# Input projections of a hybrid attention and recurrence layer by Strassen's block products

## The chip, the cores and the metric

The kernel runs on one core of one Trainium2 chip. The time is the device time of one execution in microseconds (us), as the median of several runs. TensorE (PE in the profile) does the matrix products, VectorE (DVE), ScalarE (ACT) and GpSimd (POOL) the work on elements, SyncE (SP) issues most of the DMA transfers. SBUF is the memory on the chip that all engines read, PSUM the one that TensorE writes, and DRAM lies outside.

## The reference

One layer: a combined input projection of 2048 tokens, two groups of heads that work on its columns, an output projection with a residual and a layer norm.

```python
h = jnp.einsum('btd,de->bte', h_res, w_in[layer])          # 2048 x 1024 by 1024 x 3328
hq, hf, hi, hg, aq, ak, av, ag = jnp.split(h, IN_SPLITS, axis=-1)
f = lb + (1.0 - lb) * jax.nn.sigmoid(hf)
o_h = hgrn2_chunk(rs(silu(hq)), rs(1.0 - f), rs(hi), rs(jnp.log(f)))   # 4 heads of 128, chunks of 64
...                                                        # norm of o_h, times silu(hg)
q_a = partial_rope(aq ...)                                  # 8 query heads of 64
k_a = partial_rope(ak ...)                                  # 2 key/value heads
o_a = swa_with_sinks(q_a, k_a, v_a, sinks) * silu(ag)       # causal window of 128 tokens
out = jnp.einsum('bte,ed->btd', concat(o_h, o_a), w_out[layer])
z = DN_ALPHA * h_res + out
...                                                        # layer norm of z
```

All is float32. The input projection has 26 column tiles of 128: 10 for attention (kv, two q, two gate tiles for each of the two key/value heads) and 16 for the recurrence (for each of two head pairs: four tiles of forget gate and query, four of value and output gate).

## The kernel before

Each large product is done in three passes. `load_split` fetches 128x1024 of x or of a weight (L94, SyncE), ScalarE copies it to the rounded type (L97, the high part, `_h`), and VectorE or GpSimd subtracts that from the original (L98, the low part, `_l`). Then high by high, high by low and low by high are summed in PSUM. `project_t` (L104 to L112) does that for one weight tile and 512 tokens: 8 slices of the contraction, three matmuls of 128x512 each, 24 in all. `project_n` (L114 to L122) does it with tokens as rows for values and output gates (`vg`).

The work is emitted in three parts. Attention (L184 to L330) runs over the two key/value heads j and over four blocks b of 512 tokens. For each it loads and splits x, projects `kvp`, two `qp` and two `gp`, rotates keys and queries (`rotate`, L206 to L213: VectorE reads PSUM, GpSimd multiplies `sw` by the sines), and goes through four blocks of 128 tokens: scores `sp` (L270, L271), mask and maximum on VectorE (L274 to L280), exponentials on ScalarE (L283), their normalization on GpSimd (L293), four transposes `pt` (L296), two masked copies `ptb` (GpSimd L307, VectorE L317), the product with the values `op` (L320), the gate (L328), and a transfer to DRAM (`sw_spill`, L329).

The recurrence (L354 to L506) runs over two head pairs j and four blocks b. For each head it projects the forget gate `fp` (L380), takes tanh, scans and a reciprocal (`e`, `re`, L382 to L395), makes `kq` on GpSimd (L398, L399), projects the query `hq` (L405), and then goes over two pairs of 128-token blocks: `vg` by `project_n` (L427), in-chunk products `ap`, `kp` (L444, L447, L450), state products `hkv` (L475) and outputs `ho`. The weights of `vg` (`wh_4` to `wh_7`) are loaded at b = 0, with their low parts on GpSimd (L418).

The output part (L509 to L555) does the last product `po` (L537 to L539), the residual, and the norm. The order on each engine is set by a scheduler that works on the whole program; a tile that is written again waits for the readers of what it held. Products take their PSUM tiles from a ring of three (`mm`), scores from another of three (`sc`).

Of the kernel before, what the change touches and what calls it, by code (L numbers as in the profile page):

```python
# [17 lines left out]
P = 128  # L18
# [3 lines left out]
TB = 512  # L22
# [14 lines left out]


@with_exitstack
def tile_hybrid_layer(  # L40
# [17 lines left out]
    rawp = ctx.enter_context(tc.tile_pool(name="rawp", bufs=3))  # L58
    wp = ctx.enter_context(tc.tile_pool(name="wp", bufs=8))
    xp = ctx.enter_context(tc.tile_pool(name="xp", bufs=7))  # L60
# [10 lines left out]
    ]  # L71

    def mm_ps(name):
        return psp.tile([P, 512], F32, tag="mm", name=name, bufs=3)

    def sc_ps(name):
        return psp.tile([P, 512], F32, tag="sc", name=name, bufs=3)
# [9 lines left out]
    def load_split(src, pool, tag, name, scale=None, lo_eng="d", parts=1, stage=None):  # L87
        spool, stag = stage or (rawp, "raw")
        raw = spool.tile([P, 1024], F32, tag=stag, name=f"{name}_raw")
# [13 lines left out]

    def project_t(ps, w, xs):  # L104
        wh, wl = w
        for k in range(KT):
            xh, xl = xs[k // 2]
            c = slice((k % 2) * TB, (k % 2 + 1) * TB)
            r = slice(k * P, (k + 1) * P)
            nc.tensor.matmul(ps, lhsT=wh[:, r], rhs=xh[:, c], start=k == 0, stop=False)  # L110
            nc.tensor.matmul(ps, lhsT=wh[:, r], rhs=xl[:, c], start=False, stop=False)  # L111
            nc.tensor.matmul(ps, lhsT=wl[:, r], rhs=xh[:, c], start=False, stop=k == KT - 1)  # L112
# [69 lines left out]
    hk = ctx.enter_context(tc.tile_pool(name="shared", bufs=2))  # L182
    early = [hk.tile([P, NBLK, 129], F32, tag=f"e{h}", name=f"e{h}_0", bufs=1) for h in range(2)]
    with tc.tile_pool(name="swa", bufs=2, reuse_waits="tile") as wk:  # L184
        for j in range(2):
            wg = [None] * 5
            prev_k = prev_v = None
            for b in range(NTB):
                if j == b == 0:
                    xs = []  # L190
                    for step in ("w0", "x0", "x1", "w1", "x2", "x3", "w2"):
                        i = int(step[1])
                        if step[0] == "w":
                            st_ = (None, (wk, "gate"), (wk, "gate"))[i] if i < 3 else None
                            wg[i] = load_split(wt[i], wp, "w", f"wa0_{i}", parts=2 if i == 0 else 1, stage=st_)
                        else:
                            st_ = None if i < 2 else (hk, "q0")
                            xs.append(load_split(xt[0, i], xp, "x", f"xa0_0_{i}", parts=2, stage=st_))
                else:
                    if wg[0] is None:  # L200
                        wg[0] = load_split(wt[5 * j], wp, "w", f"wa{j}_0")
                    xs = load_x(b, f"xa{j}")
                cs = wk.tile([P, 2, TB], F32, tag="cs", name=f"cs{j}_{b}", bufs=1)
                nc.sync.dma_start(cs, rope[b])

                def rotate(ps, rows, name):  # L206
                    sw = hk.tile([P, TB], F32, tag="sw", name=f"sw_{name}")
                    rot = hk.tile([P, TB], F32, tag="rot", name=f"rot_{name}")
                    nc.vector.stream_shuffle(sw[:rows], ps[:rows], swap)
                    nc.gpsimd.tensor_mul(sw[:rows], sw[:rows], cs[:rows, 1, :])  # L210
                    nc.vector.tensor_mul(rot[:rows], ps[:rows], cs[:rows, 0, :])
                    nc.vector.tensor_add(rot[:rows], rot[:rows], sw[:rows])
                    return rot  # L213

                kvp = mm_ps(f"kvp{j}_{b}")
                project_t(kvp, wg[0], xs)
                kv = hk.tile([P, TB], F32, tag="kv", name=f"kv{j}_{b}", bufs=1)
                nc.scalar.activation(kv, kvp, AF.Copy)
                krot = rotate(kvp, 64, f"k{j}_{b}")
                kh = wk.tile([P, P + TB], F32R, tag="kh", name=f"kh{j}_{b}")  # L220
                kl = wk.tile([P, P + TB], F32R, tag="kl", name=f"kl{j}_{b}")
                if prev_k is not None:
                    for new, old in zip((kh, kl), prev_k):
                        nc.vector.tensor_copy(new[:, 0:P], old[:, TB : TB + P].bitcast(F32))
                nc.scalar.activation(kh[0:64, P:], krot[0:64], AF.Copy)
                nc.scalar.activation(kh[64:128, P:], krot[0:64], AF.Copy)
                nc.vector.tensor_sub(kl[0:64, P:], krot[0:64], kh[0:64, P:].bitcast(F32))
                nc.scalar.activation(kl[64:128, P:], kl[0:64, P:].bitcast(F32), AF.Copy)
                vt = tr_ps(f"vt{j}_{b}")
                for i in range(NBLK):  # L230
                    nc.tensor.transpose(vt[:, i, :], kv[:, i * P : (i + 1) * P], ident)
                v = wk.tile([P, NBLK, 64], F32, tag="v", name=f"v{j}_{b}")
                nc.scalar.activation(v, vt[:, :, 64:128], AF.Copy, scale=0.5)

                qs = []
                for g in range(2):
                    if wg[1 + g] is None:
                        wg[1 + g] = load_split(wt[5 * j + 1 + g], wp, "w", f"wa{j}_{1 + g}")
                    qp = mm_ps(f"qp{j}_{b}_{g}")
                    project_t(qp, wg[1 + g], xs)  # L240
                    qrot = rotate(qp, P, f"q{j}_{b}_{g}")
# [384 lines left out]
```

## Time and profile before

| | |
|---|---|
| median of three runs | 952.93 us (950.11, 952.93, 953.89) |
| span of the profiled execution | 951.3 us |
| TensorE busy | 933.0 us, 98% |
| VectorE busy | 607.3 us, 64% |
| GpSimd busy | 322.0 us, 34% |
| ScalarE busy | 308.4 us, 32% |
| DRAM read, written | 73.41 MB, 16.78 MB |

The span is the time from the first to the last recorded instruction of one execution; the runs' times are taken outside and include what lies around it. A page of the profile gives busy times over the whole span. Below it stand views of stretches (windows), of single instructions in order of time (timeline), of groups of like instructions, and the chain of work that ended last, which is followed back from the last instruction to what released it.

### The profile page before, as it was taken

What the parts mean: (1) busy time and instruction counts of PE and PEld (TensorE: products, weight loads), DVE (VectorE), ACT (ScalarE), POOL (GpSimd) and SP (SyncE); (2) the same over time, 40 slices, a digit from 0 to 9 for tenths busy, and PEclk for the clock granted to TensorE, in tenths of its full rate; (3) what the DMA queues carried; (4) which work ended last, traced back from release to release, by engine and by line L of the source; (5) the groups of instructions that cost most, each with busy time, mean ns of one, the idle gap of its engine ahead of it and who ended that gap; (6) DMA issues with size and microseconds to landing.
All of it is one profiled execution on the core that took longest, in us unless ns stands there. A gap on an engine that the chain in (4) does not pass through costs nothing.

```text
span 951.3 us, 12917 instructions
## 1 busy us (share of the span) xinstructions
PE 933.0 (98%) x4744; PEld 750.7 (79%) x4744; DVE 607.3 (64%) x1233; ACT 308.4 (32%) x785; POOL 322.0 (34%) x306
## 2 busy tenths in 40 slices
PE   8999999999998999999999999999999989999996
PEld 7878777777786777878887887888788878888885
DVE  5877887867879955726366383726458446666554
ACT  5455545544564423131142423122133211000000
POOL 1645536445447534313042642313133111111111
PEclk9999999999999999999999999999999999999998
DMA  7423243033242403002032321103013253444321
GB/s 261 165 72 123 70 158 124 33 106 106 78 151 94 127 12 101 23 12 100 1 122 78 100 100 65 47 1 102 10 56 123 78 188 134 143 152 146 113 99 57
DMA packets 33216, 91.03 MB, mean 96 GB/s; under 512 B 4224, under 2 KB 12416, under 8 KB 33152
## 3 DMA queue, kind: packets, MB, share of 16 engines
q1 hardware_dynamic: 27792, 73.41, 23.7%
q0 software_dynamic: 2912, 8.40, 2.5%
q10 hardware_dynamic: 2448, 8.39, 2.2%
q8 instruction: 37, 0.61, 0.3%
q14 instruction: 27, 0.22, 0.1%
HBM read 73.41 MB, written 16.78 MB: 95 GB/s over the span
## 4 chain that ended last, share of the span: by engine, by line
PE 85%; DVE 6%; DMA 4%; ACT 3%; issue 1%; SPq 0%; POOL 0%; POOLq 0%; DVEq 0%; ACTq 0%
PE vg L121 6%; PE vg L120 6%; PE vg L122 6%; PE po L537 6%; PE po L539 6%; PE po L538 6%; PE fp L110 3%; PE fp L111 3%; PE fp L112 3%; PE hq L112 3%; PE hq L110 3%; PE hq L111 3%; PE op L320 3%; PE qp L112 2%; PE qp L110 2%; PE qp L111 2%
## 5 line engine op out<-in xcount | busy, mean ns | idle before, releaser
L537 PE MATMUL po<-wo_h,mh 128*128 128x512 f32 (+1 forms) x264 | 103.1, 391 | 2.8 <-DVE z L540 2.8
L539 PE MATMUL po<-wo_h,ml 128*128 128x512 f32 (+1 forms) x264 | 102.0, 386 | 0.0
L538 PE MATMUL po<-wo_l,mh 128*128 128x512 f32 (+1 forms) x264 | 101.9, 386 | 0.0
L120 PE MATMUL vg<-wh_h,xh_h 128*128 128x512 f32 x256 | 100.8, 394 | 0.0
L121 PE MATMUL vg<-wh_l,xh_h 128*128 128x512 f32 x256 | 100.8, 394 | 0.0
L122 PE MATMUL vg<-wh_h,xh_l 128*128 128x512 f32 x256 | 100.7, 394 | 0.0
L98 POOL TENSOR_TENSOR xh_l<-xh_raw,xh_h 128x1024 fp32r<-128x1024 f32 x16 | 39.1, 2448 | 125.6 <-ACT xh_h L97 122.9
L540 DVE SCALAR_TENSOR_TENSOR z<-xr,po 128x512 f32<-128x512 f32 (+1 forms) x33 | 22.1, 672 | 70.3 <-PE po L539 64.3
L545 POOL TENSOR_SCALAR rs<-mv 128x1 f32<-128x1 f32 x16 | 9.4, 584 | 151.4 <-DVE mv L543 151.4
L283 ACT ACTIVATE wt<-sp,st 128x128 f32<-128x128 f32 x128 | 45.8, 365 | 44.4 <-DVE st L279 44.0
L537 PEld LDWEIGHTS po<-wo_h,mh 128*128 128x128 f32 x264 | 50.1, 190 | 12.4 <-DVE z L540 3.0
L293 POOL TENSOR_TENSOR wt<-wt,st 128x512 f32<-128x512 f32 x32 | 37.4, 1169 | 61.9 <-DVE st L292 35.2
L539 PEld LDWEIGHTS po<-wo_h,ml 128*128 128x128 f32 x264 | 50.0, 189 | 10.1
L538 PEld LDWEIGHTS po<-wo_l,mh 128*128 128x128 f32 x264 | 50.0, 189 | 9.5
L343 ACT ACTIVATE mh<-mp 128x512 fp32r<-128x512 f32 x16 | 9.6, 599 | 144.8 <-PE mp L342 144.8
L120 PEld LDWEIGHTS vg<-wh_h,xh_h 128*128 128x128 f32 x256 | 48.4, 189 | 10.1 <-issue 0.6
L121 PEld LDWEIGHTS vg<-wh_l,xh_h 128*128 128x128 f32 x256 | 48.1, 188 | 10.2 <-issue 0.6
L122 PEld LDWEIGHTS vg<-wh_h,xh_l 128*128 128x128 f32 x256 | 48.1, 188 | 9.9 <-issue 0.4
L395 DVE RECIPROCAL re<-e 128x512 f32<-128x512 f32 x16 | 53.5, 3344 | 0.0
L433 DVE SCALAR_TENSOR_TENSOR hg<-tg,vg 128x256 f32<-128x256 f32 x32 | 13.4, 420 | 60.2 <-ACT tg L431 60.2
L110 PE MATMUL fp<-xh_h,wh_h 128*128 128x512 f32 x128 | 51.2, 400 | 0.0
L110 PE MATMUL qp<-xa_h,wa_h 128*128 128x512 f32 x128 | 50.7, 396 | 0.0
(173 smaller groups left out, 2483.9 us busy)
## 6 DMA issues: line engine op xcount, KB each, us to landing
xh_raw<-in_xt_dram SPq DMA_DIRECT2D x32, 512.0 KB, 3.6
xa_raw<-in_xt_dram SPq DMA_DIRECT2D x28, 512.0 KB, 3.7
wh_raw<-in_wt_dram SPq DMA_DIRECT2D x16, 512.0 KB, 3.4
xr<-in_xn_dram SPq DMA_DIRECT2D x16, 512.0 KB, 3.6
out_dram<-y ACTq DMA_DIRECT2D x15, 512.0 KB, 2.6
wa_raw<-in_wt_dram SPq DMA_DIRECT2D x9, 512.0 KB, 4.9
cs<-in_rope_dram SPq DMA_DIRECT2D x8, 512.0 KB, 3.4
sw_spill<-mix POOLq DMA_DIRECT2D x32, 128.0 KB, 2.5
```

Source lines behind the costliest of these rows:

```text
L98: engines[lo_eng].tensor_sub(lo[:, c], raw[:, c], hi[:, c].bitcast(F32))
L110: nc.tensor.matmul(ps, lhsT=wh[:, r], rhs=xh[:, c], start=k == 0, stop=False)
L111: nc.tensor.matmul(ps, lhsT=wh[:, r], rhs=xl[:, c], start=False, stop=False)
L112: nc.tensor.matmul(ps, lhsT=wl[:, r], rhs=xh[:, c], start=False, stop=k == KT - 1)
L120: nc.tensor.matmul(ps, lhsT=xh[:, r], rhs=wh[:, c], start=k == 0, stop=False)
L121: nc.tensor.matmul(ps, lhsT=xh[:, r], rhs=wl[:, c], start=False, stop=False)
L122: nc.tensor.matmul(ps, lhsT=xl[:, r], rhs=wh[:, c], start=False, stop=k == KT - 1)
L283: nc.scalar.activation(wt_[:, s, :], sps[s // 2][:, s % 2, P:], AF.Exp, bias=st[:, 1, s : s + 1], scale=0.125, accum_out=st[:, 3, s : s + 1],)
L395: nc.vector.reciprocal(re, e[:, :, 1:129])
L537: nc.tensor.matmul(ps, lhsT=mh[:, e, :], rhs=wh[:, c], start=e == 0, stop=False)
L538: nc.tensor.matmul(ps, lhsT=mh[:, e, :], rhs=wl[:, c], start=False, stop=False)
L539: nc.tensor.matmul(ps, lhsT=ml[:, e, :], rhs=wh[:, c], start=False, stop=e == 7)
```

## The change

18 of the 26 column tiles, all of attention's ten and the eight of forget gates and queries, are paired (`PAIRS`). For a pair of tiles and a half of the tokens (1024) the product is cut in 2 by 2 blocks: contraction halves of 512, token blocks of 512, tiles of 128 columns. Strassen's scheme gives the four result blocks from seven block products, with sums of blocks of x (`s1` to `s4`, and the plain `a11`, `a12`, `a22`) and of blocks of the weights (`t1` to `t4`). Each block product is 12 matmuls of 128x512, against 8 x 12 in the plain way. Three PSUM tiles `px`, `py`, `pz` take the products; ScalarE copies their interim sums to SBUF (`snap`, L300 after the change), VectorE adds the other half (`joined`, L308), and SyncE stores each result block of 128x512 in DRAM (`proj`, 72 blocks of 256 KB).

There are 18 steps: two token halves with nine pairs each. The x factors are made once a half (`prepare_x`), 28 blocks split in high and low parts, 16 of them sums that VectorE makes; each has one buffer, so the second half's are written over the first's. The weight factors are made for each step (`prepare_w`), seven blocks; the low parts go to VectorE and GpSimd in turn. The four attention units of a half (`attend`) are emitted at steps 3 to 6 of it, and read their projections from DRAM. The recurrence starts behind all steps, reads `fp` and `qp` from DRAM and keeps `project_n` for `vg`; its pools lie in the SBUF memory that the steps' pools had. Products and scores share a ring of six PSUM tiles. Lines of the changed kernel are not those of the profile.

```diff
+PAIRS = [(0, 5), (1, 2), (3, 4), (6, 7), (8, 9), (10, 12), (11, 13), (18, 20), (19, 21)]
...
+    proj = {
+        (w, b): dram.tile([P, TB], F32, tag=f"pj{w}_{b}", name=f"proj{w}_{b}")
+        for pair in PAIRS
+        for w in pair
+        for b in range(NTB)
+    }
     def mm_ps(name):
-        return psp.tile([P, 512], F32, tag="mm", name=name, bufs=3)
+        return psp.tile([P, 512], F32, tag="mm", name=name, bufs=6)
     def sc_ps(name):
-        return psp.tile([P, 512], F32, tag="sc", name=name, bufs=3)
+        return psp.tile([P, 512], F32, tag="mm", name=name, bufs=6)
...
+        def split2(src, h, l):
+            nc.scalar.activation(h, src, AF.Copy)
+            lo_engine().tensor_sub(l, src, h.bitcast(F32))
...
+        def prepare_x(s):
...
+            def put(n, q, src):
+                h = xc.tile([P, 512], F32R, tag=f"{n}{q}h", name=f"x{s}_{n}{q}h")
+                l = xc.tile([P, 512], F32R, tag=f"{n}{q}l", name=f"x{s}_{n}{q}l")
+                split2(src, h, l)
+                made[n][q] = (h, l)
...
+            for q in range(4):
+                a21, a22 = load(1, q, f"x{s}_r21{q}"), load(1, 4 + q, f"x{s}_r22{q}")
+                a11, a12 = load(0, q, f"x{s}_q11{q}"), load(0, 4 + q, f"x{s}_q12{q}")
+                s1, s2 = tmp_tile(f"x{s}_s1{q}"), tmp_tile(f"x{s}_s2{q}")
+                nc.vector.tensor_add(s1, a21, a22)
+                nc.vector.tensor_sub(s2, s1, a11)
+                put("s2", q, s2)
+                put("s1", q, s1)
+                s3 = tmp_tile(f"x{s}_s3{q}")
+                nc.vector.tensor_sub(s3, a11, a21)
+                put("s3", q, s3)
+                s4 = tmp_tile(f"x{s}_s4{q}")
+                nc.vector.tensor_sub(s4, a12, s2)
+                put("s4", q, s4)
+                put("a22", q, a22)
...
+        def prepare_w(s, pair, raws):
+            b11, b12, b21, b22 = raws
+            w = {1: w_split(b11, f"{n}_1"), 2: w_split(b21, f"{n}_2")}
+            nc.vector.tensor_sub(t1, b12, b11)
+            nc.vector.tensor_sub(t2, b22, t1)
+            w[6] = w_split(t2, f"{n}_6")
+            w[5] = w_split(t1, f"{n}_5")
+            nc.gpsimd.tensor_sub(t3, b22, b12)
+            w[7] = w_split(t3, f"{n}_7")
+            w[3] = w_split(b22, f"{n}_3")
+            nc.gpsimd.tensor_sub(t4, b21, t2)
+            w[4] = w_split(t4, f"{n}_4")
...
+            px = mm_ps(f"px{n}")
+            product(px, w[1], x["a11"], True)
+            s1 = snap(px, "s1")
+            py = mm_ps(f"py{n}")
+            product(py, w[2], x["a12"], True)
+            joined(0, 0, py, s1)
+            product(px, w[6], x["s2"], False)
+            s2 = snap(px, "s2")
+            pz = mm_ps(f"pz{n}")
+            product(pz, w[5], x["s1"], True)
+            s5 = snap(pz, "s5")
+            product(px, w[7], x["s3"], False)
+            joined(1, 1, px, s5)
+            product(pz, w[3], x["s4"], False)
+            joined(0, 1, pz, s2)
+            product(px, w[4], x["a22"], False)
+            finish(1, 0, snap(px, "c10"))
...
-                project_t(kvp, wg[0], xs)
+            kv = fetch(0, "kvc", 1)
...
+        ready = {3: (0, 0), 4: (0, 1), 5: (1, 0), 6: (1, 1)}
+        for t, (s, pair) in enumerate(steps):
...
+            if t + 1 < len(steps):
+                ahead = load_pair(*steps[t + 1])
+                w_next = prepare_w(*steps[t + 1], ahead)
+            if t % len(PAIRS) in ready:
+                j, half = ready[t % len(PAIRS)]
+                attend(j, 2 * s + half)
+            multiply(s, pair, w, x)
...
-                    fp = mm_ps(f"fp{hd}_{b}")
-                    project_t(fp, wf[2 * h], xs)
+                    fp = hk.tile([P, TB], F32, tag="fp", name=f"fp{hd}_{b}")
+                    nc.sync.dma_start(fp, proj[10 + 8 * j + 2 * h, b])
...
-                    qp = mm_ps(f"hq{hd}_{b}")
-                    project_t(qp, wf[2 * h + 1], xs)
+                    qp = hk.tile([P, TB], F32, tag="qp", name=f"qp{hd}_{b}")
+                    nc.sync.dma_start(qp, proj[11 + 8 * j + 2 * h, b])
```

Three places show how the order moves. On VectorE near the start, before the change, low parts of weights and x stand ahead of the first rotations of key and query.

```order
L98 TENSOR_TENSOR wa_2_l<-wa_2_raw,wa_2_h 128x1024
L98 TENSOR_TENSOR wa_3_l<-wa_3_raw,wa_3_h 128x1024
L98 TENSOR_TENSOR wa_4_l<-wa_4_raw,wa_4_h 128x1024
L209 STREAM_SHUFFLE sw_k_0_277<-kvp_0_250 64x512
L211 TENSOR_TENSOR rot_k_0_278<-kvp_0_250,cs_0_248 64x512
L209 STREAM_SHUFFLE sw_q_0_0_321<-qp_0_0_296 128x512
L211 TENSOR_TENSOR rot_q_0_0_322<-qp_0_0_296,cs_0_248 128x512
L98 TENSOR_TENSOR xa_1_0_l<-xa_1_0_raw,xa_1_0_h 128x1024
L212 TENSOR_TENSOR rot_k_0_278<-rot_k_0_278,sw_k_0_277 64x512
```

After the change there stand at that place the sums of x blocks (`x_s`), low parts of factors, and the join of the first result block (`c_0_0`).

```order
L189 TENSOR_TENSOR x_a220l<-x_r_341,x_a220h 128x512
L247 TENSOR_TENSOR x_s_344<-x_s_343,xk_263 128x512
L189 TENSOR_TENSOR x_s20l<-x_s_344,x_s20h 128x512
L189 TENSOR_TENSOR x_a222l<-x_r_405,x_a222h 128x512
L251 TENSOR_TENSOR x_s_355<-xk_263,x_r_339 128x512
L308 TENSOR_TENSOR c_0_0_539<-py_0_526,s_0_0_524 128x512
L189 TENSOR_TENSOR x_s30l<-x_s_355,x_s30h 128x512
L189 TENSOR_TENSOR w_0_3l<-w_5_1_261,w_0_3h 128x512
L254 TENSOR_TENSOR x_s_361<-xk_319,x_s_344 128x512
L246 TENSOR_TENSOR x_s_375<-x_r_371,x_r_373 128x512
```

So the first steps of VectorE went from a few subtractions for one block of tokens to the whole set of factors of 1024 tokens.

On GpSimd, before the change, the low parts of the `vg` weights are made among attention's last blocks (`sw_q` of the rotation, `ptb`, `wt`, and a spill).

```order
L98 TENSOR_TENSOR wh_4_l<-wh_4_raw,wh_4_h 128x1024
L210 TENSOR_TENSOR sw_q_3_0_3058<-sw_q_3_0_3058,cs_3_2983 128x512
L307 AFFINE_SELECT ptb_8_0_2810<-wtt_8_2808 128x512
L210 TENSOR_TENSOR sw_q_3_1_3094<-sw_q_3_1_3094,cs_3_2983 128x512
L98 TENSOR_TENSOR wh_5_l<-wh_5_raw,wh_5_h 128x1024
L293 TENSOR_TENSOR wt_10_2867<-wt_10_2867,st_10_2868 128x512
L307 AFFINE_SELECT ptb_9_0_2856<-wtt_9_2854 128x512
L329 DMA sw_spill_1_89<-mix_8_2818 128x256
L98 TENSOR_TENSOR wh_6_l<-wh_6_raw,wh_6_h 128x1024
```

After the change they stand at the start of the recurrence, between `k` and `kq` of the first two blocks of tokens and low parts of x.

```order
L102 TENSOR_TENSOR xh_0_1_l<-xh_0_1_raw,xh_0_1_h 128x1024
L542 TENSOR_SCALAR k_0_5333<-thf_0_5329,nc_242,c_241 128x512
L554 TENSOR_TENSOR kq_0_5345<-k_0_5333,e_0_5291 128x4x64
L102 TENSOR_TENSOR xh_0_3_l<-xh_0_3_raw,xh_0_3_h 128x1024
L555 TENSOR_TENSOR kq_0_5345<-k_0_5333,re_0_5343 128x4x64
L102 TENSOR_TENSOR wh_4_l<-wh_4_raw,wh_4_h 128x1024
L542 TENSOR_SCALAR k_0_5362<-thf_0_5358,nc_242,c_241 128x512
L102 TENSOR_TENSOR wh_5_l<-wh_5_raw,wh_5_h 128x1024
L554 TENSOR_TENSOR kq_0_5374<-k_0_5362,e_0_5293 128x4x64
L102 TENSOR_TENSOR wh_6_l<-wh_6_raw,wh_6_h 128x1024
L555 TENSOR_TENSOR kq_0_5374<-k_0_5362,re_0_5372 128x4x64
L102 TENSOR_TENSOR wh_7_l<-wh_7_raw,wh_7_h 128x1024
```

So attention's operations no longer stand around them.

On TensorE, before the change, the first `vg` product follows the last query projection `hq` of its block.

```order
L110 MATMUL hq_0_3530<-xh_0_3_h,wh_3_h 128x512
L111 MATMUL hq_0_3530<-xh_0_3_l,wh_3_h 128x512
L112 MATMUL hq_0_3530<-xh_0_3_h,wh_3_l 128x512
L120 MATMUL vg_0_0_3585<-wh_4_h,xh_0_0_h 128x512
L121 MATMUL vg_0_0_3585<-wh_4_l,xh_0_0_h 128x512
L122 MATMUL vg_0_0_3585<-wh_4_h,xh_0_0_l 128x512
```

After the change it follows the last Strassen product (`px_19`, of the pair 19 and 21), and first pieces of two `vg` tiles stand ahead of `kp` and `ap`, which need `kq`.

```order
L292 MATMUL px_19_5168<-x_a223l,w_19_4h 128x512
L293 MATMUL px_19_5168<-x_a223h,w_19_4l 128x512
L114 MATMUL vg_0_0_5409<-wh_4_h,xh_0_0_h 128x512
L114 MATMUL vg_0_1_5440<-wh_4_h,xh_0_0_h 128x512
L608 MATMUL kp_0_0_5472<-ident,kq_0_5345 128x128
L598 MATMUL ap_0_0_5471<-kq_0_5345 64x128
L601 MATMUL ap_0_0_5471<-kq_0_5345 64x64
L115 MATMUL vg_0_0_5409<-wh_4_l,xh_0_0_h 128x512
L116 MATMUL vg_0_0_5409<-wh_4_h,xh_0_0_l 128x512
```

So the recurrence's first TensorE instructions now stand directly behind the last step of the products, with no projection of the same block in between.

## Rows read from the trace of the kernel before

**Rows 1.** The page: span, busy time of each engine, chain that ended last.
```profile
span 951.3 us, 12917 instructions
PE 933.0 (98%) x4744; PEld 750.7 (79%) x4744; DVE 607.3 (64%) x1233; ACT 308.4 (32%) x785; POOL 322.0 (34%) x306
...
PE 85%; DVE 6%; DMA 4%; ACT 3%; issue 1%; SPq 0%; POOL 0%; POOLq 0%; DVEq 0%; ACTq 0%
```
**Rows 2.** Timeline of TensorE, dense stretch: start us, duration us, engine, line, instruction.
```profile
484.04 0.40 PE L111 MATMUL fp<-xh_l,wh_h 128*128 128x512 f32 x1
...
489.06 0.39 PE L112 MATMUL fp<-xh_h,wh_l 128*128 128x512 f32 x1
```
**Rows 3.** Windows 50:300: all; L110; L296 (PE, PEld); L98 (DVE, POOL).
```profile
50.00:300.00 250.00, 248.73 (x1314) 195.22 (x1313) 198.73 (x439) 131.84 (x366) 126.82 (x108) 1.00 0.30 100
...
50.00:300.00 250.00, 103.71 (x263) 49.48 (x263) 1.00 0.30 100
...
50.00:300.00 250.00, 16.66 (x104) 12.46 (x104) 1.00 0.30 100
...
50.00:300.00 250.00, 33.24 (x21) 35.26 (x14) 1.00 0.30 100
```
A row of a window gives the stretch and its length, busy us and instructions of PE, PEld, DVE, ACT and POOL (of one line only the engines that it runs on), granted TensorE clock, DMA share, GB/s.

**Rows 4.** Window of one recurrence step, all engines.
```profile
418.70:472.80 54.10, 54.10 (x283) 43.79 (x282) 27.26 (x60) 12.86 (x34) 14.28 (x14) 1.00 0.15 49
```
**Rows 5.** Chain of work: same instruction in two steps (start us, duration us).
```profile
418.73 0.44 PE hkv L475 x4
...
472.83 0.44 PE hkv L475 x4
```
**Rows 6.** TensorE's timeline at the start; first data of x on ScalarE.
```profile
8.30 0.49 PE L110 MATMUL kvp<-xa_h,wa_h 128*128 128x512 f32 x1 [0.55 <-ACT xa_h L97]
...
14.23 0.39 PE L112 MATMUL kvp<-xa_h,wa_l 128*128 128x512 f32 x1
...
L97 ACT ACTIVATE xa_h<-xa_raw x15: 615/635/1063, 7.6 to 46.8; 128x512 fp32r<-128x512 f32 x8, 128x1024 fp32r<-128x1024 f32 x7
```
**Rows 7.** Groups by shape: busy us, mean ns of one, idle time before.
```profile
L98 DVE TENSOR_TENSOR xa_l<-xa_raw,xa_h 128x512 fp32r<-128x512 f32 x8 | 5.2, 684 | 3.8 <-ACT xa_h L97 3.8
...
L98 POOL TENSOR_TENSOR wh_l<-wh_raw,wh_h 128x1024 fp32r<-128x1024 f32 x8 | 19.6, 2449 | 0.1
...
L386 POOL TENSOR_SCALAR k<-thf,nc,c 128x512 f32<-128x512 f32 x16 | 19.0, 1188 | 38.5 <-ACT thf L382 38.5
...
L398 POOL TENSOR_TENSOR kq<-k,e 128x256 f32<-128x256 f32 x16 | 13.4, 835 | 25.5 <-DVE e L392 25.4
...
L97 ACT ACTIVATE xh_h<-xh_raw 128x1024 fp32r<-128x1024 f32 x32 | 33.7, 1059 | 26.5 <-DMA xh_raw<-in_xt_dram 22.0 <-PE vg L121 4.5
```
**Rows 8.** Timeline of VectorE and GpSimd, 25 to 33 us.
```profile
25.09 2.76 POOL L210 TENSOR_TENSOR sw_q<-sw_q,cs 128x512 f32<-128x512 f32 x1
...
26.61 1.78 DVE L212 TENSOR_TENSOR rot_k<-rot_k,sw_k 64x512 f32<-64x512 f32 x1
27.79 4.59 POOL L98 TENSOR_TENSOR xa_l<-xa_raw,xa_h 128x1024 fp32r<-128x1024 f32 x1
28.31 0.68 DVE L212 TENSOR_TENSOR rot_q<-rot_q,sw_q 128x512 f32<-128x512 f32 x1
28.92 1.21 DVE L98 TENSOR_TENSOR xa_l<-xa_raw,xa_h 128x1024 fp32r<-128x1024 f32 x1
```
**Rows 9.** A wait of TensorE in its timeline, and the window behind it.
```profile
309.79 0.38 PE L270 MATMUL sp<-kh,q 128*128 128x256 f32 x1 [1.85 <-ACT wt L283]
...
310.80:314.20 3.40, 3.40 (x11) 2.82 (x11) 3.04 (x7) 3.40 (x5) 3.11 (x3) 0.50 0.13 49
```
**Rows 10.** DMA issues: count, KB each, median us from issue to landing.
```profile
sw_spill<-mix POOLq DMA_DIRECT2D x32, 128.0 KB, 2.5
```

More of the change, by code (lines that the diff above doesn't have):

```diff
@@ L57, in tile_hybrid_layer @@
     const = ctx.enter_context(tc.tile_pool(name="const", bufs=1))
-    rawp = ctx.enter_context(tc.tile_pool(name="rawp", bufs=3))
-    wp = ctx.enter_context(tc.tile_pool(name="wp", bufs=8))
-    xp = ctx.enter_context(tc.tile_pool(name="xp", bufs=7))
     psp = ctx.enter_context(tc.tile_pool(name="psp", bufs=2, space=PSUM))
@@ L85, in tile_hybrid_layer, with load_split @@
     engines = {"d": nc.vector, "p": nc.gpsimd}
-    def load_split(src, pool, tag, name, scale=None, lo_eng="d", parts=1, stage=None):
-        spool, stag = stage or (rawp, "raw")
-        raw = spool.tile([P, 1024], F32, tag=stag, name=f"{name}_raw")
+    def load_split(src, pool, tag, name, scale=None, lo_eng="d", parts=1):
+        raw = rawp.tile([P, 1024], F32, tag="raw", name=f"{name}_raw")
         hi = pool.tile([P, 1024], F32R, tag=f"{tag}h", name=f"{name}_h")
@@ L102, in load_x @@
         return [load_split(xt[b, j], xp, "x", f"{name}_{b}_{j}", lo_eng=LO_ENGINES[j]) for j in range(4)]
[L104 to L112, printed above, removed]
     def project_n(ps, ws, xs, blk):
@@ L351, in load_wo @@
         return load_split(wo[e], pool, tag, f"wo{e}", scale=hgw_s[:, e : e + 1] if e < 4 else None)
+    late = ctx.enter_context(ExitStack())
+    rawp = late.enter_context(tc.tile_pool(name="rawp", bufs=3, reuse_waits="tile"))
+    wp = late.enter_context(tc.tile_pool(name="wp", bufs=8, reuse_waits="tile"))
+    xp = late.enter_context(tc.tile_pool(name="xp", bufs=7, reuse_waits="tile"))
     with (
@@ L357, in tile_hybrid_layer @@
     ):
-        es = [[early[h], wk1.tile([P, NBLK, 129], F32, tag=f"e{h}", name=f"e{h}_1")] for h in range(2)]
+        hk = wk
+        es = [
+            [wk1.tile([P, NBLK, 129], F32, tag=f"e{h}_{i}", name=f"e{h}_{i}") for i in range(2)] for h in range(2)
+        ]
         ats = [wk1.tile([P, 4, P], F32, tag=f"at{i}", name=f"at{i}") for i in range(2)]
@@ L364, in tile_hybrid_layer @@
         for j in range(2):
-            wf = [None] * 4
             wv = None
@@ L369, in tile_hybrid_layer @@
             for b in range(NTB):
-                if b == 0:
-                    wf[0] = load_split(wt[10 + 8 * j], wp, "w", f"wh{j}_0")
                 xs = load_x(b, f"xh{j}")
@@ L376, in tile_hybrid_layer @@
                     e = es[h][b % 2]
-                    if b == 0 and h == 1:
-                        wf[2] = load_split(wt[10 + 8 * j + 2], wp, "w", f"wh{j}_2")
-                    fp = mm_ps(f"fp{hd}_{b}")
-                    project_t(fp, wf[2 * h], xs)
+                    fp = hk.tile([P, TB], F32, tag="fp", name=f"fp{hd}_{b}")
+                    nc.sync.dma_start(fp, proj[10 + 8 * j + 2 * h, b])
                     th = hk.tile([P, TB], F32, tag="th", name=f"thf{hd}_{b}", bufs=2)
@@ L400, in tile_hybrid_layer @@
                     kn.append(knh)
-                    if b == 0:
-                        wf[2 * h + 1] = load_split(wt[10 + 8 * j + 2 * h + 1], wp, "w", f"wh{j}_{2 * h + 1}")
-                    qp = mm_ps(f"hq{hd}_{b}")
-                    project_t(qp, wf[2 * h + 1], xs)
+                    qp = hk.tile([P, TB], F32, tag="qp", name=f"qp{hd}_{b}")
+                    nc.sync.dma_start(qp, proj[11 + 8 * j + 2 * h, b])
                     tq = hk.tile([P, TB], F32, tag="th", name=f"thq{hd}_{b}", bufs=2)
@@ L613 @@
     from concourse.bass_utils import run_bass_kernel_spmd as _run
-    nc = _bacc.Bacc("TRN2", target_bir_lowering=False, num_devices=1)
+    nc = _bacc.Bacc("TRN2", target_bir_lowering=False, num_devices=1, dynamic_dma_scratch_size=4096)
     arrays, args = {}, []
```

355 lines of the change are left out of this document (213 added, 142 removed).

## The prediction

> **What bounds the kernel now.** I read the page's head first: TensorE is busy 98% of the 951.3 us span, and the chain that ended last is TensorE for 85% [rows 1]. So fewer TensorE instructions shorten the run at once, as long as no other engine becomes late in the stage where they go. Then I read the stages apart, since the 64% of VectorE is a mean. In 50 to 300 us (attention) VectorE is busy 79% and GpSimd 51% [rows 3]. A recurrence step of one head pair and 512 tokens lasts 418.73 to 472.83, 54.1 us [rows 5], with TensorE busy throughout and VectorE at 27.26 us, 50% [rows 4]. The three runs have a median of 952.93, 1.6 us over the profiled span; the sum is made on the span and 1.6 is added.
>
> **What the change removes.** Before, a tile of 512 tokens takes 24 matmuls of 128x512; the 18 tiles over 2048 tokens take 1728. After, a pair of tiles over 1024 tokens takes seven products of 12: 18 x 84 = 1512. The order of the instructions shows both counts. In a dense stretch 22 matmuls start between 484.04 and 489.06, 0.228 us each [rows 2]. Removed: 216 x 0.228 = **49.2 us**. Everything else in the change adds.
>
> **Loss at the start.** Before, the first matmul starts at 8.30 and the dense run at 14.23, when 12 had been done: 14.23 - 12 x 0.228 = 11.5 us lost [rows 6]. After, the first step needs factors made from sums. VectorE's order holds 41 operations of 512 columns with two SBUF inputs ahead of the join that ends the second result block, at 0.684 each [rows 7], 28 us, and some 4.5 us that read PSUM or are small; GpSimd holds 21 subtractions at half of 2.449 [rows 7], 25.7 us. The first data is there for ScalarE at 7.6 [rows 6]. If the two engines ran side by side, the join would come at 7.6 + 32.5 = 40 us. But the timeline shows them in each other's way [rows 8]: GpSimd's `xa_l` takes 4.59 us, where a subtraction of that size has a mean of 2.449 [rows 7], while two VectorE operations with two SBUF inputs run, and VectorE's `rot_k` 1.78, against 0.68 for the wider `rot_q`, while GpSimd's `sw_q` is open. Added one behind the other they give 7.6 + 28 + 25.7 = 61 us. I take 50: part of GpSimd's work can wait beside VectorE's own waits for ScalarE and PSUM. TensorE has 83 matmuls, 18.9 us, to do by then. 50 - 18.9 - 11.5 = **+20** (40 gives +10; 61 gives +31; +5 if the next steps' products fill in more).
>
> A rule of the Trainium skill speaks to this (SBUF — State Buffer, section "SBUF: two separate sides"): VectorE and GpSimd share one pair of SBUF ports as an exclusive lock held for a whole instruction, and a VectorE operation with two SBUF inputs takes it against a GpSimd operation that reads SBUF. The trace agrees [rows 8]: the excess of `xa_l`, 2.14 us, is about the 1.89 of the two VectorE operations beside it. By the rule alone the start would cost +31, by free engines +10.
>
> **Loss at the second half of the tokens.** The x factors are single-buffered, so those of step 9 can be written only when step 8's products have read the old ones. From the join of step 8 to that of step 9 VectorE has 35 such operations and four joins, 26.5 us, and GpSimd 16 at 1.22, 19.5; TensorE has 85 matmuls, 19.4 us. Side by side TensorE waits 26.5 - 19.4 = 7 us; one behind the other 43.4 - 19.4 = 24. I take **+12**.
>
> **Attention between the products.** In 50 to 300 us TensorE's 263 recorded first-of-three matmuls stand for 789, 180 us; the other (250 - 180) us belong to 104 / 4 = 26 blocks of 128 tokens, 2.69 each [rows 3]. VectorE's 198.73 less 33.24 of subtractions is 6.36 a block, GpSimd's 126.82 less 35.26 is 3.52 [rows 3]. After, the 16 blocks of each half are spread over about six steps. TensorE: 6 x 84 x 0.228 + 16 x 2.69 = 158 us. VectorE: 16 x 6.36 = 102, and 8.5 operations a step for weights and joins, 35: 137, or 87%, where it was 79%. GpSimd: 56, and five and a half subtractions a step at 1.22, 40: 96, 61%. VectorE stays below TensorE on average and passes it in the two steps where most blocks lie. Reading `rotate` and the gate from SBUF instead of PSUM adds two-input operations that meet GpSimd's. At the lower end nothing is lost; at the upper, VectorE's 137 and half of the 65 us of its two-input work blocked give 170, so 12 a half. I take **+8** for both halves (0 to +24).
>
> **Entry to the recurrence.** Before, the split weights of the value and gate projection are made by GpSimd between attention and forget-gate work (the order shows them 10 to 15 rows ahead of need). After, only recurrence inputs come from DRAM, so these projections are the first TensorE work, and GpSimd stands ahead of the last of their weights with two x splits and four weight splits at 2.449, two `k` at 1.188, and four `kq` at 0.835 [rows 7]: 20.4 us. It starts some 3 us in (three casts of 1.06 [rows 7] by ScalarE). TensorE has about 48 matmuls, 11 us, that need only what is there. 23.4 - 11 = 12.4, with a collision or two **+14** (11 to 21). Late x tiles lie in memory that the last products read, so their loads can't come earlier.
>
> **Recurrence steps.** 54.1 - 96 x 0.228 = 32.2 us of TensorE work remain, against 27.3 of VectorE [rows 4]: 85%. In the steps VectorE, ScalarE and GpSimd form a serial chain (tanh, log, scan, reciprocal) that a fp or hq projection used to cover. I take **+3** (0 to +16).
>
> **The clock.** At 309.79 TensorE waited 1.85 us, and the next 3.40 us ran at a granted clock of 0.50, the 1.2 GHz level [rows 9]: half of 3.40, 1.7 us, lost behind a wait. With the many waits above I take **+5** (0 to +12).
>
> **DRAM round trip.** A 128 KB spill lands 2.5 us after its issue [rows 10]. A result is read a step or more (19 us) after its store, so I take 0; a fetch that waits for its store holds later weight loads on SyncE's queue, up to +10. Nothing below zero: no transfer of the old form on TensorE's path goes away.
>
> **Sum.** -49.2 + 20 + 12 + 8 + 14 + 3 + 5 = +12.8. Span 951.3 + 12.8 = 964.1, time **965.7**, say 966.
>
> **Rivals.** (1) *Cover holds*: the engines run side by side, other steps' products fill the waits. Then +8 at the start, +5, 0, +11, 0, +2: -49.2 + 26 = -23, 930 us. For it: TensorE has several PSUM banks (six in one ring) and interleaves steps; against it: [rows 8]. It decides from where the new idle sums to under 49. (2) *The losses are each a bit under my values*, +14, +8, +4, +13, +1, +4 = 44: 949 to 956. (3) *One behind the other everywhere*, the exclusive ports as the only rule: +31 +24 +20 +20 +8 +8 = 111, so 1015 us. The joins and factor sums make it the worst of all in the starts of both halves. (4) *It doesn't do what it says*: excluded by the counts 1512 and 1728.
>
> **How the numbers follow.** My forecast (958 to 985) has 0.42, the case around no change 0.14, side by side 0.30, one behind the other 0.14. A difference under 0.5% (948.2 to 957.7) is about what can't be told from no change. Faster 0.30, same 0.14, slower 0.56. The range takes most of rival 1 and stops short of rival 3: 925 to 1000.
>
> **What would show it.** TensorE's first step ending at 50 rather than 40 or 61 us; idle time ahead of the products with `s1`, `s2` at step 9; GpSimd subtractions lengthened beyond 1.3 us where VectorE is dense; TensorE waiting for GpSimd's `wh_l` ahead of the first `vg`; VectorE at 85 to 90% between; recurrence steps of 32 to 34 us; granted clock 0.50 behind each wait. I am wrong on the faster side if those two starts cost under 15 us together, and on the slower side if VectorE's attention work, not its average, holds TensorE in the steps between.

## The result, and the profile after

The changed kernel takes 1051.76 us (1050.40 to 1054.15) against 953.41: a ratio of 1.1052, interval 1.1025 to 1.1079. It is slower, as forecast, but by 98 us where I had 13, and beyond the end of my range (925 to 1000). The page of the kernel after, where [rows 1] stand for before (share of the span in brackets):

```profile
span 1048.4 us, 13652 instructions
...
PE 927.4 (88%) x4528; PEld 730.5 (70%) x4528; DVE 772.5 (74%) x1393; ACT 400.3 (38%) x1000; POOL 475.8 (45%) x419
...
PE 31%; DVE 6%; issue 3%; POOL 2%; DMA 2%; ACT 2%; POOLq 0%; DVEq 0%; ACTq 0%
```

Three numbers give the balance. TensorE is idle for 1048.4 - 927.4 = 121.0 us, where it was 18.3: +102.7. The removed matmuls should have lowered its busy time by 49.2, to 883.8; it is 927.4, so the same work took 43.6 us more. And 102.7 + 43.6 - 49.2 = 97.1, the difference of the spans. The windows by stage show both parts (us, busy us and instructions of PE, PEld, DVE, ACT, POOL, granted TensorE clock, DMA share, GB/s): first step, rest of the first token half, first step of the second half, rest of it, entry to the recurrence, recurrence, output.

```profile
0.00:64.50 64.50, 38.15 (x117) 27.12 (x118) 47.27 (x58) 26.81 (x49) 41.27 (x40) 0.68 0.42 143
64.50:296.00 231.50, 209.46 (x1019) 163.76 (x1018) 172.69 (x321) 114.57 (x310) 128.93 (x107) 0.98 0.38 123
296.00:333.50 37.50, 23.55 (x61) 13.56 (x61) 31.35 (x37) 17.28 (x32) 22.69 (x14) 0.64 0.48 161
333.50:557.00 223.50, 208.05 (x1015) 160.83 (x1013) 160.85 (x313) 105.29 (x291) 115.03 (x100) 0.98 0.34 112
557.00:600.00 43.00, 23.70 (x96) 17.37 (x97) 40.53 (x57) 19.23 (x28) 32.03 (x24) 0.76 0.59 198
600.00:857.60 257.60, 241.25 (x1362) 195.20 (x1360) 211.62 (x428) 99.39 (x257) 109.38 (x99) 0.97 0.36 117
857.60:1048.40 190.80, 183.27 (x866) 152.64 (x864) 108.16 (x183) 17.74 (x37) 26.48 (x35) 0.99 0.37 128
```

TensorE is idle and slow at once in three places: granted clock 0.68, 0.64 and 0.76, where before the clock fell to 0.50 for 3.4 us behind a wait [rows 9]. The joins of the first step, VectorE's sums that end a result block, come at 60.43 and 64.49 us:

```profile
60.43 0.69 DVE L308 TENSOR_TENSOR c<-px,s 128x512 f32<-128x512 f32 x1 [3.26 <-PE px L293]
64.49 0.69 DVE L308 TENSOR_TENSOR c<-pz,s 128x512 f32<-128x512 f32 x1 [3.36 <-PE pz L293]
```

TensorE's timeline ahead of them:

```profile
25.99 0.39 PE L293 MATMUL px<-x_s20h,w_6l 128*128 128x512 f32 x1
32.28 0.79 PE L291 MATMUL pz<-x_s11h,w_5h 128*128 128x512 f32 x1 [5.90 <-ACT x_s11h L188]
...
40.28 0.79 PE L292 MATMUL pz<-x_s12l,w_5h 128*128 128x512 f32 x1 [1.35 <-POOL x_s12l L189]
...
57.33 0.63 PE L293 MATMUL px<-x_s31h,w_7l 128*128 128x512 f32 x1
57.75 0.63 PE L291 MATMUL px<-x_s32h,w_7h 128*128 128x512 f32 x1
...
60.40 0.40 PE L291 MATMUL px<-x_a111h,w_1h 128*128 128x512 f32 x1
60.63 0.40 PE L292 MATMUL px<-x_a111l,w_1h 128*128 128x512 f32 x1
```

After a wait of 5.90 us for a factor the products come in pieces of one to three, with waits between; they start 0.43 us apart (57.33 to 57.75), against 0.228 in [rows 2]. The clock was back at full at 60 us only (60.40 to 60.63, 0.23 apart). The same stretch on all engines shows what the factors wait for:

```profile
36.69 0.62 ACT L188 ACTIVATE x_s41h<-x_s 128x512 fp32r<-128x512 f32 x1
36.73 0.69 DVE L246 TENSOR_TENSOR x_s<-x_r,x_r 128x512 f32<-128x512 f32 x1
36.87 1.69 POOL L189 TENSOR_TENSOR x_s31l<-x_s,x_s31h 128x512 fp32r<-128x512 f32 x1 [1.38 <-ACT x_s31h L188]
...
37.34 1.76 DVE L189 TENSOR_TENSOR x_s41l<-x_s,x_s41h 128x512 fp32r<-128x512 f32 x1
...
38.52 1.71 POOL L189 TENSOR_TENSOR x_s12l<-x_s,x_s12h 128x512 fp32r<-128x512 f32 x1
39.02 1.75 DVE L247 TENSOR_TENSOR x_s<-x_s,xk 128x512 f32<-128x512 f32 x1
```

VectorE's 0.68 us operations take 1.75 where a GpSimd subtraction is open, and the GpSimd ones 1.7: the picture of [rows 8], now in row after row.

### The profile page after: what moved, and what is told of

Read it like the earlier page. It is cut to its first block, busy times and chain, and to the rows that moved or that the text cites. A ratio compares the mean times of both kernels' runs of the same rounds, so it can differ in the third digit from the quotient of the medians.

```text
span 1048.4 us, 13652 instructions
## 1 busy us (share of the span) xinstructions
PE 927.4 (88%) x4528; PEld 730.5 (70%) x4528; DVE 772.5 (74%) x1393; ACT 400.3 (38%) x1000; POOL 475.8 (45%) x419
## 5 line engine op out<-in xcount | busy, mean ns | idle before, releaser
L114 PE MATMUL vg<-wh_h,xh_h 128*128 128x512 f32 x256 | 105.7, 414 | 12.8 <-ACT wh_h L101 12.8
L115 PE MATMUL vg<-wh_l,xh_h 128*128 128x512 f32 x256 | 103.8, 406 | 0.0
L116 PE MATMUL vg<-wh_h,xh_l 128*128 128x512 f32 x256 | 103.0, 402 | 0.0
L114 PEld LDWEIGHTS vg<-wh_h,xh_h 128*128 128x128 f32 x256 | 50.3, 197 | 22.9 <-ACT wh_h L101 13.2
L115 PEld LDWEIGHTS vg<-wh_l,xh_h 128*128 128x128 f32 x256 | 50.3, 196 | 10.3 <-issue 0.3
L426 POOL TENSOR_TENSOR wt<-wt,st 128x512 f32<-128x512 f32 x32 | 42.4, 1326 | 32.6 <-DVE st L425 19.3
L403 PE MATMUL sp<-kh,q 128*128 128x256 f32 (+1 forms) x128 | 36.9, 313 | 15.9 <-DVE q L380 6.8
L102 POOL TENSOR_TENSOR xh_l<-xh_raw,xh_h 128x1024 fp32r<-128x1024 f32 x16 | 38.9, 2435 | 24.4 <-ACT xh_h L101 24.3
L101 ACT ACTIVATE xh_h<-xh_raw 128x1024 fp32r<-128x1024 f32 x32 | 33.2, 1052 | 21.5 <-DMA xh_raw<-in_xt_dram 19.4
L403 PEld LDWEIGHTS sp<-kh,q 128*128 128x128 f32 x128 | 25.2, 197 | 23.0 <-DVE q L380 8.6
```

Source lines behind the costliest of these rows:

```text
L114: nc.tensor.matmul(ps, lhsT=xh[:, r], rhs=wh[:, c], start=k == 0, stop=False)
L115: nc.tensor.matmul(ps, lhsT=xh[:, r], rhs=wl[:, c], start=False, stop=False)
L116: nc.tensor.matmul(ps, lhsT=xl[:, r], rhs=wh[:, c], start=False, stop=k == KT - 1)
L403: nc.tensor.matmul(sp[:, h, lo:], lhsT=lhs, rhs=kh[:, kc], start=True, stop=False)
L426: nc.gpsimd.tensor_mul(wt_, wt_, st[:, 4, :].unsqueeze(2).to_broadcast([P, 4, P]))
```

## The experiments

Times beside them are medians; the changed kernel is 1051.8, the kernel before 950 to 953 beside each run.

**Plain products in the same plan.** The difference to the changed kernel:

```diff
-            product(px, w[1], x["a11"], True)
-            s1 = snap(px, "s1")
...
-            finish(1, 0, snap(px, "c10"))
+            for row in range(2):
+                for col in range(2):
+                    ps = mm_ps(f"p{row}{col}_{n}")
+                    product(ps, w[11 + col], x[f"a{row + 1}1"], True)
+                    product(ps, w[21 + col], x[f"a{row + 1}2"], False)
+                    finish(row, col, snap(ps, f"c{row}{col}"))
```

> The changed kernel with the plain eight block products in place of Strassen's seven: four x factors (a11, a12, a21, a22) and four weight factors, no sums, no joins on VectorE; halves, steps, stores to DRAM and fetches stay. TensorE gets its 216 matmuls back, +49 us by 0.228 each. Theory A (making the seven factors on VectorE and GpSimd is what costs, with the clock behind the waits): most of the losses in the starts of both halves and between the attention blocks go, about 75 us, so 1025 us (1000 to 1035). Rival B (the detour through DRAM and the separate phases cost): the losses stay, 1085 to 1100.

Measured 1060.9 (ratio 1.1152, 1.1122 to 1.1183). That is between the theories, and in neither range: of the 49 us that TensorE gets back to do, only 9 show, so in this plan making the factors costs about 40. But this kernel has exactly the matmuls of before and is 109 us slower. So the plan around the products loses that much without Strassen's scheme, and I had priced it at 14 + 3.

**The second start.** `if t == 0:` in place of `if t % len(PAIRS) == 0:` ahead of `prepare_x`. The second half's products are then made from the first half's tokens; the values are not the layer's.

> The changed kernel with the x factors of the first token half used for the second half too (it leaves out the 28 splits and 16 sums of the second half and the wait for their buffers). Theory A: the 13 us of TensorE's waits near 300 to 325 us and about 6 to 8 us of work at the low clock there go, so 1031 us (1025 to 1037). Rival (VectorE's total work sets the pace of the whole half, and the wait only moves): 1045 or more.

Measured 1020.5: 31.3 us less, more than the theory had (its range began at 1025). The second start's window is dense and at full clock then (290 to 330 us):

```profile
290.00:330.00 40.00, 38.14 (x169) 30.93 (x168) 19.68 (x27) 16.16 (x30) 17.44 (x13) 1.00 0.37 121
```

**The detour through DRAM.** `proj[...]` in the fetches replaced by blocks of `xt`.

> The changed kernel with attention and recurrence fetching blocks of the input x of the same size in place of the stored projections, so that no fetch waits for a product or a store (the values are not the layer's; the stores stay). Theory A: VectorE's waits for fetches (qc 14.5 us, kvc 4.3 us) are partly in the shadow of other waits, 1042 us (1032 to 1050). Rival B (the round trip through DRAM is the cause): under 1010.

Measured 1051.9: no change. Rival B falls; the small gain that I expected (1032 to 1050) didn't come either, so VectorE's waits for fetches lie beside others. The stores stay in this run, and so does the fetches' place behind them on SyncE's queue.

**Low parts on one engine.** `lo_engine` returns VectorE always, then GpSimd always.

> The changed kernel with the low parts of all factors on VectorE, none on GpSimd. If the two engines take turns at SBUF, a subtraction costs 0.68 us of the common time instead of 1.25 to 1.7: the first step's joins come at about 55 instead of 60 and 64 us, VectorE gets about 3.5 x 0.68 us more a step where attention lies; together 1045 us (1030 to 1060). If they run side by side, VectorE's queue grows by some 80 subtractions, 55 us, most of it late: 1075 or more.

> The changed kernel with the low parts of all factors on GpSimd. Taking turns at SBUF, each of the 77 that move costs 1.25 us or more of the common time instead of 0.68: 1080 us (1065 to 1110). Side by side, VectorE would be freed of 55 us in its dense stretches: 1025 to 1045.

Measured 1039.5 and 1064.5, the second just under its bounds. The first one's page:

```profile
PE 930.6 (89%) x4528; PEld 731.9 (70%) x4528; DVE 777.9 (75%) x1484; ACT 400.2 (38%) x1000; POOL 350.7 (34%) x328
```

VectorE has 91 instructions more, some 62 us at 0.68, and is busy only 5.4 us longer. By that estimate about 56 us of its busy time in the changed kernel was waiting for GpSimd, as the operations of 1.75 us above show it singly. The Trainium skill states that the two engines share one pair of SBUF ports as an exclusive lock, held for a whole instruction (SBUF — State Buffer, section "SBUF: two separate sides"); the trace agrees, 1.75 us for an operation that meets an open subtraction and 0.68 otherwise. Only 12 us of it reach the end. The joins of the first step come earlier by 7.4 and 8.8 us:

```profile
53.00 0.69 DVE L308 TENSOR_TENSOR c<-px,s 128x512 f32<-128x512 f32 x1 [3.50 <-PE px L293]
55.68 0.69 DVE L308 TENSOR_TENSOR c<-pz,s 128x512 f32<-128x512 f32 x1 [1.39 <-PE pz L293]
```

**Without attention blocks.** The loop over the four blocks writes a product of gate and q in place of the attention output.

> The changed kernel without the attention blocks of 128 tokens (no scores, mask, exponentials, transposes, value products); the rotations, splits of q and k, gates and fetches stay. That takes 32 x 2.69 = 86 us of TensorE work away. Theory A (TensorE loses its time among the attention blocks, where scores wait for q, exponentials and PSUM): the losses between the two starts, some 50 us above those of before, go too, 915 us (900 to 930). Rival C (factors and joins set the pace of the steps by themselves): only the 86 us and little more go, 945 to 966.

Measured 973.5, so 78 us: less than the work taken out. Theory A, that the time goes among the blocks because of the blocks, falls. Rival C holds in part (the time is 8 us over its range): with nothing else to do, TensorE now waits for the steps' own factors. A wait of it, on all engines:

```profile
152.11 1.64 DVE L380 TENSOR_TENSOR q<-rot_q,q 64x512 fp32r<-64x512 f32 x1
...
153.17 1.70 POOL L189 TENSOR_TENSOR w_4l<-w_t,w_4h 128x512 fp32r<-128x512 f32 x1
...
154.95 1.59 POOL L282 TENSOR_TENSOR w_t<-w,w_t 128x512 f32<-128x512 f32 x1
155.46 1.64 DVE L345 TENSOR_TENSOR rot_q<-qc,cs 128x512 f32<-128x512 f32 x1
...
157.19 0.69 DVE L346 TENSOR_TENSOR rot_q<-rot_q,sw_q 128x512 f32<-128x512 f32 x1
157.92 0.63 ACT L379 ACTIVATE q<-rot_q 64x512 fp32r<-64x512 f32 x1 [5.23 <-DVE rot_q L346]
...
159.22 0.63 ACT L188 ACTIVATE w_1h<-w 128x512 fp32r<-128x512 f32 x1
...
159.91 0.79 PE L291 MATMUL px<-x_a110h,w_1h 128*128 128x512 f32 x1 [7.62 <-ACT w_1h L188]
```

ScalarE's cast of the weight `w_1h` stands behind the cast of `q`, which waits 5.23 us for VectorE's rotation; VectorE's operations take 1.64 there, beside GpSimd's. TensorE pays 7.62 us for an operation of attention that it doesn't need yet.

**Filling the waits.** In the first step of each half, behind each three matmuls with `s1` and `s2`:

```diff
+                for _ in range(fill):
+                    nc.tensor.matmul(filler[0], lhsT=wh[:, r], rhs=xh, start=True, stop=True)
```

> The changed kernel with 112 additional matmuls of 128x512 whose result nobody reads, seven behind each third matmul of the products with s1 and s2 in the first step of each half, to keep TensorE at work in the short waits there. At full clock they take 25 us, about what TensorE waits in these two places. If the low clock there comes from the waits: 53 matmuls at 0.43 instead of 0.23 at the start and about as many at the second place come back at full pace, 18 us less, and 5 to 10 us of the filling stand on the path: 1042 us (1034 to 1050). If the low clock isn't caused by the waits, or the filling isn't hidden: 1060 to 1077.

Measured 1051.2, in neither range. In the same two stretches as above the clock rises from 0.68 and 0.64 to 0.84 and 0.86:

```profile
0.00:64.50 64.50, 41.98 (x156) 32.42 (x157) 47.06 (x57) 27.31 (x48) 40.90 (x40) 0.84 0.38 134
296.00:333.50 37.50, 28.39 (x103) 21.35 (x103) 33.92 (x36) 18.33 (x33) 23.54 (x15) 0.86 0.45 152
```

So the low clock does come from TensorE's waits, and 25 us of useless work cost nothing; but the factors arrive no earlier, and nothing is gained. In these two places the low clock is the companion of the wait rather than a price on top.

**Two buffers for attention.** In the plain form, `bufs=2` for `sw`, `rot`, `kh`, `kl`, `q`, `gate`, `th`, `gc`.

> The kernel with the plain eight products (1060.9 us), with two buffers instead of one for attention's sw, rot, kh, kl, q, gate, th and gc, which is what the kernel before has; the memory is that of the twelve x factors that the plain way doesn't need. Theory A1 (single buffers chain the attention units behind each other): the 72 us that TensorE loses in the attention stretches, against 11 before, fall by half or more, 1015 us (990 to 1030). Rival (ring of PSUM tiles, or the fetches): 1050 to 1062.

Measured 1064.0: theory A1 falls, as long as the ring of PSUM tiles is common; no run has two buffers and separate rings.

**Rings of PSUM tiles.** Two rings of three instead of one of six:

```diff
     def sc_ps(name):
-        return psp.tile([P, 512], F32, tag="mm", name=name, bufs=6)
+        return psp.tile([P, 512], F32, tag="sc", name=name, bufs=3)
```

and `bufs=3` in `mm_ps`; in the changed kernel, in the plain form, and the other way round in the kernel before.

> The changed kernel with two rings of three PSUM tiles (products, scores) in place of one ring of six, as the kernel before had. Theory A2 (scores stand in the ring behind product tiles that wait for ScalarE and VectorE): 1030 us (1015 to 1042). Rival (the ring of six lets two steps overlap and is worth having): 1055 to 1080.

> The kernel with the plain eight products (1060.9 us), with separate rings of three PSUM tiles for products and scores. Theory A2 (in a common ring a product takes its place behind scores that wait for the exponentials, so TensorE can't run ahead): TensorE's waits for wt and c in the attention stretches, 36 us, and some 20 us in the recurrence go: 1015 us (1000 to 1030). Rival (the latency of the attention chain itself, with fewer projections to cover it): 1040 or more.

> The kernel before, with one ring of six PSUM tiles for products and scores in place of two rings of three, and nothing else changed. Theory A2 (in a common ring a product stands behind scores that wait for ScalarE, wherever products and scores lie side by side): it loses about what separate rings gave back to the plain eight products (64 us): 1005 us (985 to 1020). Rival (the ring hurts only with the fetches and the separate phases of the changed kernel): 950 to 960.

Measured 1027.4 (-24.4), 996.9 (-64.0) and 1012.2 against 949.6 (ratio 1.0657, 1.0640 to 1.0675): the common ring alone costs the kernel before 62.6 us, with no other edit. About 64 were expected, and the rival, that the ring hurts only in the new plan, falls. In the kernel before and in the plain form it is the largest single item; in the changed kernel the second start (31.3) is larger. TensorE's waits in the kernel before with the ring of six (total us, times, longest):

```profile
PE sp L270 <- ACT wt L283: 30.3, 8, 6.1
PE hkv L475 <- ACT kt L459: 10.3, 15, 0.7
PE sp L270 <- DVE gate L256: 4.7, 2, 2.9
```

and in the kernel before as it was, where `sp` waited for `wt` for

```profile
PE sp L270 <- ACT wt L283: 2.2, 2, 1.8
```

A score tile now waits for exponentials eight times, up to 6.1 us, and whatever stands behind it on TensorE's queue waits along. The edit changes more than places: the order on TensorE moves with it. Counted in the traces, the 32 score matmuls of each unit of 512 tokens stand together (8 runs of 32, with only transposes and value products among them); in the kernel before as it was they were spread over the projections in 39 runs of 4 to 12. So six of a unit's eight score tiles fill the ring, the seventh waits for the exponentials of one of them, and the next projection stands behind. With the common ring:

```profile
133.92 0.28 PE L271 MATMUL sp<-kl,q 128*128 128x256 f32 x1
138.49 0.54 PE L270 MATMUL sp<-kh,q 128*128 128x256 f32 x1 [4.30 <-ACT wt L283]
...
141.27 0.79 PE L110 MATMUL kvp<-xa_h,wa_h 128*128 128x512 f32 x1 [0.74 <-ACT wt L283]
```

and in the kernel before as it was, where a projection follows its scores at once:

```profile
135.55 0.28 PE L271 MATMUL sp<-kl,q 128*128 128x256 f32 x1
135.67 0.40 PE L110 MATMUL qp<-xa_h,wa_h 128*128 128x512 f32 x1
```

How much is due to the places and how much to the order that follows from them, no run tells apart. In the changed kernel most of the 24 us lie in the recurrence: from the first to the last `vg` 282.6 us go by, with separate rings 262.5.

**The entry to the recurrence.** Loads of x and weights alternate, six raw tiles instead of three, low parts in turn.

> The changed kernel with the entry to the recurrence eased: the loads of the first x and of the value and gate weights alternate, their ring of raw tiles has six places instead of three, and the low parts of the weights go to GpSimd and VectorE in turn. The entry lost 27 us (idle and low clock, 557 to 600 us). If loads and the low parts on GpSimd set it: 1040 us (1034 to 1045). Rival (the chain tanh, scan, reciprocal, kq ahead of the first ap and kp sets it): 1047 to 1055.

Measured 1057.6 (1050.6 to 1061.0): no gain, and above the rival's range too. The wait of 12.8 us for `wh_h` fell to 6.6 in two, and TensorE's waits of `hkv` for `kt` rose from 7.2 to 15.9. That loads and GpSimd's low parts set the entry is refuted; that the chain sets it is left to the next runs.

**Three edits together**, then two variants of it.

> The changed kernel with three edits together: separate rings of three PSUM tiles (alone -24 us), low parts of the factors on VectorE (alone -12 us), and the eased entry to the recurrence. If the effects add: 1004 us (995 to 1014). If they are parts of one wait: 1015 to 1030.

> The kernel with the three edits (998.0 us: separate rings, low parts on VectorE, eased entry), with the x factors of the first token half used for the second too. The second start still loses 27 us there (225 to 320 us, idle and low clock). If the factors alone cause it: 973 us (966 to 980). If VectorE's other work takes their place: 985 to 995.

> The kernel with the three edits (998.0 us), with the kq products of the first recurrence step on VectorE in place of GpSimd. TensorE's first wait there is 9.0 us for kq from GpSimd, with vg standing behind it. If GpSimd's speed sets it: 992 us (988 to 995). If it is the chain tanh, scan, reciprocal, kq after the last products, whoever does it: 996 to 1000.

Measured 998.0, 972.1 and 999.3. The three edits give 53.8 us, more than the 37 of rings and low parts alone. The second start still costs 25.8. The entry isn't set by GpSimd's speed: with `kq` on VectorE nothing changes, the wait is 8.6 us instead of 9.0. The timeline in the kernel with the three edits:

```profile
501.63 7.86 SPq L304 DMA_DIRECT2D proj<-c  x3
509.58 0.38 SPq L542 DMA_DIRECT2D fp<-proj  x1
...
512.08 1.08 PE L453 MATMUL op<-ptb,v 128*64 128x256 f32 x8 [1.20 <-DVE mix L461]
...
512.38 0.63 ACT L544 ACTIVATE thf<-fp 128x512 f32<-128x512 f32 x1 [1.83 <-DMA fp<-proj]
...
517.02 3.34 DVE L557 RECIPROCAL re<-e 128x512 f32<-128x512 f32 x1
...
520.44 1.67 POOL L561 TENSOR_TENSOR kq<-k,re 128x256 f32<-128x256 f32 x1 [2.80 <-DVE re L557]
...
522.17 0.47 PE L612 MATMUL kp<-ident,kq 128*128 128x128 f32 x1 [9.01 <-POOL kq L561]
```

The first `kp` ends a chain (tanh, scan, reciprocal, `kq`) of 10 us that starts when `fp` is fetched, and nothing is left to cover it. The fetch is issued at 509.58, right behind the last step's stores on SyncE's queue, although the `fp` of the first tokens was made in the first half of the steps. No run fetches it earlier, so whether the queue, or the memory that the recurrence takes over from the steps, holds it stays open.

Put side by side with separate PSUM rings, the plain form takes 996.9 and Strassen's 1027.4, 30 us more. So with separate rings Strassen's seven products save 49 us and cost about 80. Of the 77 us that the changed kernel then still loses (1027.4 against 950.5), these 30 are Strassen's and some 45 lie in the plan. No version ran faster than the kernel before.

## Why the prediction was wrong

**Bound and removed work**: the count is right, 4744 TensorE instructions before and 4528 after, 216 fewer. The 49.2 us stand in the balance above as they were forecast, and 43.6 is what remains beside them; what failed is the rest of the sum.

**Start**: mechanism right, size wrong. I took 50 us for the join, between 40 and 61; the two joins came at 60.43 and 64.49. TensorE had started 81 recorded matmuls of 512 columns by then, 18.5 us; 64.5 - 18.5 - 11.5 = 34.5, not 20. The step that failed is the middle value: [rows 8] showed the two engines taking turns, so the end for one behind the other was the nearer row, and even that had no low clock in it. With the low parts on VectorE alone the last join came at 55.68, which bears out that the two engines' taking turns is a part of it.

**Second start**: +12 forecast, 31 measured (26 in the kernel with three edits). I see the same reason, but the run takes out the splits and sums together with the wait, and doesn't show it apart.

**Attention between the products**: +8 forecast; TensorE was idle 22.0 and 15.5 us in the two stretches behind the starts (64.5 to 296 and 333.5 to 557), where before it was idle 1.3 us in 250 [rows 3]. I looked for VectorE's total; what counts in the traces is what stands behind a wait on the same engine: products behind a score, a cast of a weight behind a cast of q.

**The rings**: the term that is missing. I read "six in one ring" in the diff and put it down as something in favour of the change, with no price. This is the step of the prediction that failed outright: it stood at nothing, for no reason that a row gave, and the runs show 62.6 us in the kernel before, 64.0 in the plain form and 24.4 in the changed one. An edit in two lines went in with no row and no bound, while I worked out every subtraction.

**Entry**: +14 forecast; the stage from 557 to 600 has 19.3 us idle and a clock of 0.76. I priced GpSimd's low parts, but easing them changed nothing. The timeline points to the chain of the first step without a projection beside it, which stood in my working as "+3" for the recurrence; that is argued from the trace, not shown by a run that shortens it.

**Recurrence**: +3 forecast; 16.4 us of idle time behind the entry (600 to 857.6), where [rows 4] showed none. Separate rings take 20 us off the recurrence.

**Clock**: +5 forecast. TensorE's work took 43.6 us more than at full pace. In the stretches that the traces give at 0.50, TensorE is busy 80.2 us after the change and 9.5 before; half of the difference, 35 us by estimate, is the clock's, seven times my figure. I counted waits as single events with 1.7 us each; where they lie close together the clock stays low for the whole stretch, 32 to 60 us at the start. It doesn't add to the waits as I had it: in the two places that were filled, a higher clock gave nothing back.

**DRAM round trip**: 0 forecast, 0 measured for fetches that wait for their data. What fetches lose behind stores on SyncE's queue, as `fp` at the entry, wasn't measured.

**Sum and rivals.** My terms gave +62 of losses; there were 147. With separate rings there are still some 125, so the ring alone isn't the miss: the starts, the entry, the work between and the clock were taken too small beside it. The sign doesn't hang on the ring either, as that kernel is slower by 77. Rival 3 (all one behind the other, 1015 us) was nearest, and still 12 us under the changed kernel with separate rings. Rival 2's own sum, 44 of losses, gives 948, just under the 949 to 956 that I wrote for it. Not settled: how the remaining difference of the plain form with separate rings to the kernel before, 45 us, divides; its entry with a wait of 13.2 us for `wh_h` is a part of it, and in the changed kernel an edit there only moved the wait.

## What to carry to other kernels

Price every line of a diff, the two-line ones first: a ring of buffers that two kinds of users share is a change of the order in which everything waits. When a large stage of matmuls is made shorter by elementwise work on two other engines, add their times if the trace shows that they block each other, and look at the places where no other work covers them, the start and each restart. And test a plan with the plain arithmetic first: here the plain products in the new plan told in one run that 109 us were lost without Strassen's scheme.

## What was not expected of the hardware

112 matmuls put into waits of TensorE cost no time (1051.2 against 1051.8), and raised the granted clock of these stretches from 0.68 to 0.84 and from 0.64 to 0.86. VectorE's recorded busy time holds its waits for GpSimd: 91 instructions more on it, and 5.4 us more busy, once GpSimd no longer made low parts.
